# Experts of a mixture layer: a second feature block straight to PE in fp32, and GpSimd's share of the low parts cut to the first five

## The chip, the cores and the metric

The kernel runs on one core of a Trainium2 chip. The metric is the device time of one execution in microseconds. Before the change the median of three runs is 3178.11 us (3177.04 to 3182.73).

The engines are named as in the profile: PE is TensorE (matmuls; PEld is its loading of weights), DVE is VectorE, ACT is ScalarE, POOL is GpSimd, and SP issues nearly all DMAs from one queue in order.

## The reference

The model is a first block (a state-space mixer and a mixture of experts) followed by a second block of two layers, on 512 tokens of 1024 features, all in fp32. The change touches the experts of the first block alone:

```python
def expert_choice_ffn(xn, router_w, w_gate, w_up, w_down):
    ...
    gate, idx = lax.top_k(aff, cap)
    xg = jax.vmap(lambda xs, ix: xs[ix])(xn, idx)
    hid = jax.nn.silu(jnp.einsum('becd,edf->becf', xg, w_gate)) * jnp.einsum('becd,edf->becf', xg, w_up)
    y = jnp.einsum('becf,efd->becd', hid, w_down) * gate[..., None].astype(xn.dtype)
    ...
```

There are 16 experts; each picks 64 tokens. Each has three weight matrices of 1024 x 1024 in fp32, w_gate, w_up and w_down. All 48 matrices are read once: 48 x 4 MB.

## The kernel before

**Precision.** Most matmuls are made of fp32r operands, a shorter form of fp32. So that nothing is lost, an fp32 operand is split into two parts: high = the operand cast to fp32r (by ACT), low = operand minus high (by DVE or GpSimd). Products of the parts are added up in PSUM.

**Stages.** A mixer, its output projection with the router (`w_o`, `route`), then the experts (`experts`, line 1086), then the second block (`b2_entry`, `layer`). The order of the instructions on each engine is made by a planner that simulates the program when the kernel is built (`schedule_with_timeline_sim`); in the experts no order is written out by hand, apart from a dependency that holds a few early loads behind the gather of the first tokens.

**The experts.** The loop in `experts` takes expert after expert. For expert e it calls `hidden(e)` (gate and up matrices, silu, product), then `finish(e - 1)`, which calls `down` for the expert before. After every odd expert `pair_rows` and, after experts 1, 5, 9 and 13, `combine` add the results of the pairs to the residual rows `h`. For every even expert `xs_pair` transposes the gathered tokens of the next pair and `gather` fetches those of the one after it.

**One matrix, eight feature blocks.** A matrix is taken in eight blocks k = 0 to 7 of 128 input features x 1024 output features, 512 KB each (`moe_mm`, line 1007). All 384 blocks of the stage come in one fixed order. `moe_load` (line 929) issues the load of the next block into one of 19 raw buffers in rotation: seven `mraw`, three `raw`, four `PT`, four in `rawx`, one in `moewk`. A load waits on SP's queue until the last reader of its buffer is done.

`moe_w` (line 943) prepares a block. A block whose k is in `DIRECT` (line 26: k = 2) is handed to PE as it is. Any other is split: ACT casts the high part (L955) and an engine subtracts for the low part (L957). That engine is GpSimd for the first five split blocks and for every ninth after them (`MPOOL`, line 27), else DVE. High and low parts have four buffers each, three `whi`/`wlo` and one `mwhi`/`mwlo`. Then the next load is issued.

`moe_mm` has the matmuls. The stationary operand of a split block holds 64 columns of high and 64 columns of low parts of the tokens (`XS` for gate and up, `HS` for down), so that two matmuls on each half of 512 output features give all four products: one with the block's high part (L1017), one with its low part (L1018). A direct block has one plain fp32 matmul on each half (L1015), whose stationary operand is the 64 tokens in fp32 (`XD` for gate and up, the tile `hs` for down), and it issues its next load after them. In the trace each plain fp32 matmul has two records. Both kinds add into the same PSUM rows:

```python
                if wl is None:
                    nc.tensor.matmul(pp[q][0:64], X32[k], wh[:, c], start=False, stop=False)
                    continue
                nc.tensor.matmul(pp[q], X[:, k], wh[:, c], start=k == 0, stop=False)
                nc.tensor.matmul(pp[q], X[:, k], wl[:, c], start=False, stop=k == 7)
            if wl is None:
                self.moe_load()
```

At the end of a gate or up matrix ACT copies PSUM out (L1031, L1032) and PE multiplies by a constant matrix J (L1035), which adds the high and low rows and transposes. At the end of a down matrix ACT copies the low rows (L1055) and DVE adds them (L1056). `xs_pair` transposes (L996) and splits the tokens (ACT L1003, DVE L1004), and ACT copies block 2 of them to `XD` (L1001).

Of the kernel before, what the change touches and what calls it, by code (L numbers as in the profile page):

```python
# [22 lines left out]
MRAW = 7  # L23
AFTER = (0, 1, 2, 3)
RAWS = MRAW + 12
DIRECT = (2,)
MPOOL = 9
GROUPS = (1, 5, 9, 13)
CAP = 64
EPS = 1e-6  # L30
# [7 lines left out]
class Net:  # L38
# [904 lines left out]
    def moe_w(self, *key):  # L943

        nc = self.nc
        got, raw = self.raws.pop(0)
        assert got == key
        if key[2] in DIRECT:
            return raw, None
        n = self.cw  # L950
        self.cw += 1
        P, tag, bufs = (self.wp, "w", 3) if n % 4 < 3 else (self.mw, "mw", 1)
        hi = P.tile([128, 1024], F32R, name=tag + "hi", tag=tag + "hi", bufs=bufs)
        lo = P.tile([128, 1024], F32R, name=tag + "lo", tag=tag + "lo", bufs=bufs)
        nc.scalar.copy(hi, raw)  # L955
        eng = nc.gpsimd if n < 5 or n % MPOOL == MPOOL - 1 else nc.vector
        eng.tensor_tensor(lo, raw, hi.bitcast(F32), OP.subtract)  # L957
        self.moe_load()
        return hi, lo
# [27 lines left out]
    def xs_pair(self):  # L987

        nc, mo = self.nc, self.mo2
        XS = [mo.tile([128, 8, 128], F32R, name="XS%d" % i, tag="XS", bufs=3) for i in range(2)]  # L990
        XD = mo.tile([128, max(1, len(DIRECT)), 2, 64], F32, name="XD", tag="XD", bufs=2)
        for q in range(2):
# [5 lines left out]
            ks = slice(4 * q, 4 * q + 4)  # L998
            for j, k in enumerate(DIRECT):
                if k // 4 == q:  # L1000
                    nc.scalar.copy(XD[:, j], p4[:, k % 4])  # L1001
            for i in range(2):
                nc.scalar.copy(XS[i][:, ks, 0:64], p4[:, :, i])  # L1003
                nc.vector.tensor_tensor(XS[i][:, ks, 64:128], p4[:, :, i], XS[i][:, ks, 0:64].bitcast(F32), OP.subtract)  # L1004
        return [(XS[i], {k: XD[:, j, i] for j, k in enumerate(DIRECT)}) for i in range(2)]

# [16 lines left out]
    def hidden(self, e, X):  # L1023
# [19 lines left out]
        V.tensor_tensor(HS[:, :, 64:128], s3, HS[:, :, 0:64].bitcast(F32), OP.subtract)  # L1043
        return HS, {k: s3[:, k] for k in DIRECT}

# [1030 lines left out]
```

## Time and profile before

| | before |
|---|---|
| median of three runs | 3178.11 us (3177.04 to 3182.73) |
| the profiled execution | 3183.61 us, of which the span from the first to the last instruction 3181.8 us |
| mean granted TensorE clock over the span | 0.981 of full speed |
| PE, DVE, ACT, POOL busy | 96%, 71%, 50%, 12% of the span |
| split blocks in the experts | 336, of which 294 low parts by DVE and 42 by POOL |
| direct blocks in the experts | 48 |

The profile shows one execution. An engine's busy time is the union of its records; matmuls are pipelined, so the records of neighbours overlap and a matmul's duration is longer than what it adds to the time. An arrow `<-` behind an idle time names the instruction whose end released the one that waited. A tile's name stands without its buffer's number; `mm<-wlo,XS` is a matmul into the tile `mm` that reads `wlo` and `XS`.

### The profile page before, as it was taken

How to read it: one execution, taken by the hardware profiler on the slowest of the kernel's cores; microseconds unless marked ns; L12 is line 12 of the kernel's file. 1: busy time of each engine (PE TensorE's matmuls, PEld its weight loads, DVE VectorE, ACT ScalarE, POOL GpSimd, SP SyncE). 2: the span in 40 equal slices, each digit the busy share in tenths (PEclk: the TensorE clock that was granted, in tenths of full speed). 3: DMA queues.
4: the chain of work that ended last, by engine and by line, in shares of the span. 5: the costliest groups of instructions: out<-in, count | busy, mean ns of one | idle time of the engine just before them, and what ended most of it. 6: DMA issues, size and time to landing. Idle time of an engine off the chain costs nothing. (4 is left out here: it accounts for less than half of the span.)

```text
span 3181.8 us, 43471 instructions
## 1 busy us (share of the span) xinstructions
PE 3039.0 (96%) x16242; PEld 2477.6 (78%) x16242; DVE 2247.8 (71%) x3782; ACT 1587.9 (50%) x2711; POOL 379.9 (12%) x295
## 2 busy tenths in 40 slices
PE   7999999969999999699999999999999999999998
PEld 4888777756655666678787789998878777789986
DVE  7778665468988888777565488873676655688854
ACT  6445432228766776365353435551465444445541
POOL 1454200032112121200011000000000011000000
PEclk9999999979999999899999999999999999999999
DMA  5112245549999997311215333332312224333332
GB/s 196 54 47 71 83 143 192 198 179 396 374 345 342 350 370 271 101 62 58 87 56 166 97 117 99 109 105 93 106 54 74 76 93 148 100 106 107 107 100 79
DMA packets 140781, 470.05 MB, mean 148 GB/s; under 512 B 16269, under 2 KB 20365, under 8 KB 140569
## 3 DMA queue, kind: packets, MB, share of 16 engines
q1 hardware_dynamic: 139416, 463.08, 41.7%
q0 software_dynamic: 1152, 4.19, 0.4%
q8 instruction: 127, 2.08, 0.3%
q14 instruction: 86, 0.70, 0.1%
HBM read 456.71 MB, written 10.50 MB: 147 GB/s over the span
## 5 line engine op out<-in xcount | busy, mean ns | idle before, releaser
L107 DVE TENSOR_TENSOR wlo<-raw,whi 128x1024 fp32r<-128x1024 f32 (+4 forms) x340 | 379.9, 1120 | 306.4 <-ACT whi L106 305.0
L106 ACT CAST whi<-raw 128x1024 fp32r<-128x1024 f32 (+4 forms) x340 | 317.6, 936 | 416.7 <-PE mm L116 165.0
L115 PE MATMUL mm<-xTh,whi 128*128 128x512 f32 (+2 forms) x880 | 344.7, 392 | 5.6 <-ACT P L1245 2.6
L116 PE MATMUL mm<-xTh,wlo 128*128 128x512 f32 (+3 forms) x880 | 341.3, 388 | 0.0
L117 PE MATMUL mm<-xTl,whi 128*128 128x512 f32 (+2 forms) x880 | 339.1, 386 | 0.4 <-DVE xTl L267 0.2
L115 PE MATMUL mm<-whi,xTh 128*128 128x512 f32 (+1 forms) x536 | 208.1, 390 | 2.5 <-DVE zt L562 2.1
L116 PE MATMUL mm<-whi,xTl 128*128 128x512 f32 (+1 forms) x536 | 208.2, 389 | 0.5 <-DVE xTl L1150 0.5
L117 PE MATMUL mm<-wlo,xTh 128*128 128x512 f32 (+1 forms) x536 | 204.7, 387 | 0.0
L115 PEld LDWEIGHTS mm<-xTh,whi 128*128 128x128 f32 (+1 forms) x880 | 165.8, 188 | 46.5 <-ACT P L1245 4.2
L117 PEld LDWEIGHTS mm<-xTl,whi 128*128 128x128 f32 (+1 forms) x880 | 165.4, 188 | 36.9 <-DVE xTl L267 1.5
L116 PEld LDWEIGHTS mm<-xTh,wlo 128*128 128x128 f32 (+1 forms) x880 | 165.9, 189 | 34.3 <-issue 1.4
L1018 PE MATMUL mm<-wlo,XS 128*128 128x512 f32 x336 | 114.3, 413 | 18.0 <-DVE wlo L957 11.7
L1409 POOL TENSOR_TENSOR ql<-q,qh 128x512 fp32r<-128x512 f32 x16 | 20.7, 1291 | 853.0 <-ACT qh L1408 853.0
L115 PEld LDWEIGHTS mm<-whi,xTh 128*128 128x128 f32 x536 | 102.1, 191 | 23.4 <-DVE zt L562 2.5
L116 PEld LDWEIGHTS mm<-whi,xTl 128*128 128x128 f32 x536 | 102.1, 191 | 20.3 <-DVE xTl L1150 1.0
L117 PEld LDWEIGHTS mm<-wlo,xTh 128*128 128x128 f32 x536 | 102.0, 190 | 19.7
L957 DVE TENSOR_TENSOR wlo<-mraw,whi 128x1024 fp32r<-128x1024 f32 x82 | 108.6, 1341 | 8.9 <-ACT whi L955 7.7
L1017 PE MATMUL mm<-whi,XS 128*128 128x512 f32 x336 | 111.2, 406 | 0.9 <-ACT whi L955 0.9
L955 ACT CAST whi<-mraw 128x1024 fp32r<-128x1024 f32 x96 | 97.7, 1049 | 15.2 <-PE mm L1017 12.5
L1245 ACT ACTIVATE P<-mm,smv 128x512 f32<-128x512 f32 x128 | 88.1, 690 | 31.2 <-DVE P L1533 16.1
L107 DVE TENSOR_TENSOR flo<-fs,fhi 128x1024 fp32r<-128x1024 f32 x80 | 97.6, 1220 | 5.7 <-ACT fhi L106 4.6
L116 PE MATMUL mm<-whi,hl 128*128 128x512 f32 x248 | 96.6, 390 | 0.0
(827 smaller groups left out, 8620.3 us busy)
## 6 DMA issues: line engine op xcount, KB each, us to landing
raw<-w_f SPq DMA_DIRECT2D x92, 512.0 KB
raw<-w_gate SPq DMA_DIRECT2D x68, 512.0 KB
mraw<-w_gate SPq DMA_DIRECT2D x52, 512.0 KB
mraw<-w_down SPq DMA_DIRECT2D x49, 512.0 KB
araw<-ada SPq DMA_DIRECT2D x48, 512.0 KB
mraw<-w_up SPq DMA_DIRECT2D x43, 512.0 KB
rawu<-w_f SPq DMA_DIRECT2D x40, 512.0 KB
PT<-w_up SPq DMA_DIRECT2D x30, 512.0 KB
```

The lines of the kernel that those rows point to most:

```text
L106: nc.scalar.copy(hi[:, :n], raw[:, :n])
L107: nc.vector.tensor_tensor(lo[:, :n], raw[:, :n], hi[:, :n].bitcast(F32), OP.subtract)
L115: mm(out, ah, bh, start=first, stop=False)
L116: mm(out, al, bh, start=False, stop=False)
L117: mm(out, ah, bl, start=False, stop=last)
L955: nc.scalar.copy(hi, raw)
L957: eng.tensor_tensor(lo, raw, hi.bitcast(F32), OP.subtract)
L1017: nc.tensor.matmul(pp[q], X[:, k], wh[:, c], start=k == 0, stop=False)
L1018: nc.tensor.matmul(pp[q], X[:, k], wl[:, c], start=False, stop=k == 7)
L1245: nc.scalar.activation(P, s, AF.Exp, bias=v[:, 8 + i:9 + i], accum_out=v[:, 16 + i:17 + i])
L1409: nc.gpsimd.tensor_tensor(ql, q, qh.bitcast(F32), OP.subtract)
```

## The change

`DIRECT` names a second block, k = 6, so that two of the eight blocks of each matrix go to PE unsplit. `xs_pair` and `hidden` take the list as it is, so `XD` grows to two blocks for each expert of a pair, and ACT makes one more copy for each pair. The constant `MPOOL` goes, and with it GpSimd's every ninth low part: GpSimd keeps the first five, and all others are DVE's.

```diff
-DIRECT = (2,)
-MPOOL = 9
+DIRECT = (2, 6)
...
         nc.scalar.copy(hi, raw)
-        eng = nc.gpsimd if n < 5 or n % MPOOL == MPOOL - 1 else nc.vector
+        eng = nc.gpsimd if n < 5 else nc.vector
         eng.tensor_tensor(lo, raw, hi.bitcast(F32), OP.subtract)
         self.moe_load()
         return hi, lo
```

## Rows read from the trace of the kernel before

**Rows 1.** The page, busy time of each engine over the span.

```profile
PE 3039.0 (96%) x16242; PEld 2477.6 (78%) x16242; DVE 2247.8 (71%) x3782; ACT 1587.9 (50%) x2711; POOL 379.9 (12%) x295
```

**Rows 2.** Busy time by stretches: us, busy (instructions) per engine, PEclk, DMA share, GB/s.

```profile
core 0: us, PE busy (x) PEld busy (x) DVE busy (x) ACT busy (x) POOL busy (x), PEclk, DMA share, GB/s
720.00:760.00 40.00, 39.51 (x190) 28.01 (x189) 35.07 (x37) 33.23 (x44) 9.06 (x4) 1.00 1.01 394
705.00:1275.00 570.00, 534.88 (x2284) 357.03 (x2284) 486.04 (x490) 412.21 (x510) 114.62 (x45) 0.99 0.92 347
```

**Rows 3.** Timeline, PE, 899 to 917 us: start, us, what.

```profile
899.78 0.63 PE L1017 MATMUL mm<-whi,HS 128*128 128x512 f32 x2
...
903.05 0.63 PE L1018 MATMUL mm<-wlo,XS 128*128 128x512 f32 x2
903.62 1.93 PE L1015 MATMUL mm<-mraw,XD 128*64 128x512 f32 x4
905.48 0.72 PE L1017 MATMUL mm<-whi,XS 128*128 128x512 f32 x2
...
906.51 0.63 PE L1017 MATMUL mm<-whi,XS 128*128 128x512 f32 x2
...
909.32 1.10 PE L1017 MATMUL mm<-whi,XS 128*128 128x512 f32 x4
911.89 0.73 PE L1018 MATMUL mm<-wlo,XS 128*128 128x512 f32 x2 [1.48 <-DVE wlo L957]
...
915.81 1.10 PE L1035 MATMUL aux<-J,moewk 128*128 128x64 f32 x8
916.73 0.71 PE L1017 MATMUL mm<-whi,XS 128*128 128x512 f32 x2
```

**Rows 4.** Groups of PE, 705 to 1275 us: busy, mean ns, idle before and its releasers.

```profile
L1018 PE MATMUL mm<-wlo,XS 128*128 128x512 f32 x336 | 114.3, 413 | 18.0 <-DVE wlo L957 11.7 <-POOL wlo L957 5.8
...
L1035 PE MATMUL aux<-J,moewk 128*128 128x64 f32 x512 | 64.0, 272 | 1.3 <-ACT moewk L1031 1.3
L1018 PE MATMUL mm<-wlo,HS 128*128 128x512 f32 x168 | 56.6, 408 | 2.8 <-DVE wlo L957 2.1 <-POOL wlo L957 0.7
...
L1018 PE MATMUL mm<-mwlo,XS 128*128 128x512 f32 x112 | 38.5, 415 | 3.1 <-DVE mwlo L957 1.6 <-POOL mwlo L957 1.3
...
L1015 PE MATMUL mm<-mraw,XD 128*64 128x512 f32 x48 | 23.2, 605 | 0.0
L1082 PE MATMUL aux<-yh,oht 128*128 128x512 f32 x56 | 20.8, 406 | 2.2 <-DVE h L1115 1.2 <-ACT yh L1066 1.1
...
L1018 PE MATMUL mm<-mwlo,HS 128*128 128x512 f32 x56 | 18.9, 414 | 1.5 <-DVE mwlo L957 1.4
...
L996 PE MATMUL aux<-ident,moewk 128*128 128x128 f32 x64 | 10.2, 295 | 4.9 <-DMA moewk<-xf_scratch,idx 4.9
...
L1071 PE MATMUL aux<-posT,s 16*64 16x512 f32 x32 | 8.6, 612 | 0.0
...
L976 PE MATMUL aux<-vals,OH 128*128 128x6 f32 x28 | 4.4, 261 | 0.0
```

**Rows 5.** Timeline of POOL, DVE and PE at two GpSimd subtracts.

```profile
907.95 2.80 POOL L957 TENSOR_TENSOR wlo<-PT,whi 128x1024 fp32r<-128x1024 f32 x1 [10.82 <-ACT whi L955]
...
908.80 3.04 DVE L957 TENSOR_TENSOR wlo<-PT,whi 128x1024 fp32r<-128x1024 f32 x1 [0.30 <-ACT whi L955]
...
1020.93 5.71 POOL L957 TENSOR_TENSOR wlo<-mraw,whi 128x1024 fp32r<-128x1024 f32 x1 [11.42 <-ACT whi L955]
...
1026.69 2.07 PE L1018 MATMUL mm<-wlo,XS 128*128 128x512 f32 x4 [3.95 <-POOL wlo L957]
```

**Rows 6.** DVE's subtracts in the experts: two groups, and one with min/median/max ns.

```profile
L957 DVE TENSOR_TENSOR wlo<-mraw,whi 128x1024 fp32r<-128x1024 f32 x82 | 108.6, 1341 | 8.9 <-ACT whi L955 7.7 <-ACT hs L1038 1.0
...
L957 DVE TENSOR_TENSOR mwlo<-moewk,mwhi 128x1024 fp32r<-128x1024 f32 x4 | 8.9, 2228 | 1.1 <-ACT mwhi L955 1.1
...
L957 DVE TENSOR_TENSOR wlo<-mraw,whi x82: 1203/1216/3427, 714.4 to 1270.6; 128x1024 fp32r<-128x1024 f32 x82
```

**Rows 7.** What SP's queue waited for, 705 to 1275 us: total us, times, longest.

```profile
SPq L941 <- PE mm L1015: 57.3, 37, 5.3
```

## The prediction, made before the changed kernel had run

> **What bounds the kernel now.** I read the page's busy shares first. PE is busy for 96% of the span, DVE for 71%, GpSimd for 12% [rows 1]. But a share over the whole span says little here: the change touches the experts alone, so I went on to the stretch of 705 to 1275 us, in which all 384 blocks of the experts' weights are used [rows 2]. There PE is busy for 534.9 of 570 us, DVE for 486.0, ACT for 412.2, GpSimd for 114.6. The reader is to see two things in that row: PE is the bound, with little room, and DVE comes close behind, close enough to make PE wait.
>
> Next, what one block costs PE. Matmuls overlap in the records, so I count from start to start, not by durations. Seven pairs of ordinary matmuls lie between 899.78 and 903.05 us [rows 3]: 3.27 / 7 = 0.467 us a pair, 0.2335 us each. A **split block** has four of them (high and low part, two halves): 0.934 us. A **direct block** stands between a pair that starts at 903.05 and two pairs that end at 906.51: 3.46 us, less three pairs of 0.467, leaves 2.06 us. Its own four records take 1.86 us (903.62 to 905.48); the other 0.2 us are at its two edges, where weights aren't loaded ahead. So a direct block costs PE more than two split ones.
>
> The Trainium skill, "FP8 and Floating Point Precision", section "TensorE Precision Notes", says that true fp32 takes four passes through the array. That speaks against the change, which spends PE time where PE is the bound; four passes for two fp32 matmuls against one pass for each of four fp32r ones would be a factor of two, and by that alone a block would add 0.934 us. The trace agrees and shows 0.2 us on top [rows 3].
>
> Then PE's account of the stretch [rows 4]. The matmuls on the low parts stand in four groups, 336 + 168 + 112 + 56 = 672, and there are as many on the high parts: 1344 x 0.2335 = 313.8 us. Forty-eight direct blocks (k = 2 of 16 experts and three matrices): 98.9. The 512 matmuls with J, eight of which take 0.92 us (915.81 to 916.73) [rows 3]: 58.9. The combine has 56 with yh and as many with yl: 26.2. Three small groups are busy for 8.6 + 10.2 + 4.4 us with overlap; I take 18. Sum 516. **So PE waits for about 54 of the 570 us.** The idle time recorded ahead of the matmuls on the low parts adds up to 16.8 us released by DVE and 7.8 by GpSimd [rows 4], 24.6 of the 35.1 us (570 - 534.9) of recorded idle, or 70%. I spread the 54 alike: 38 us are waits for a low part (26 by DVE, 12 by GpSimd), 16 are others.
>
> Why DVE is late: its subtract takes 1216 ns in the median but up to 3427 [rows 6]. The long ones lie beside GpSimd's: one of 3.04 us starts inside a GpSimd subtract of 2.80 us, and PE then stands for 1.48 us; elsewhere GpSimd needs 5.71 us for one block and PE stands for 3.95 us [rows 3, 5]. The ten groups of DVE's low parts (294 of them; the first and the last are shown) are busy for 390.0 us in sum [rows 6]; at 1216 ns they would take 357.5. So 32.5 us of DVE's time is lost beside GpSimd.
>
> **The change, part by part.** *Block 6 direct.* Forty-eight more direct blocks in place of split ones: 48 x (2.06 - 0.934) = **+54 us** of PE work, all of it on the path that sets the end. ACT loses 48 casts and gains eight small copies (XD for block 6), DVE loses subtracts; none of this ends last by itself, it counts only through PE's waits.
>
> *GpSimd.* It now makes the low parts of blocks n < 5 and of every ninth; 37 of the latter go. Of the 336 - 48 = 288 split blocks left, DVE makes 283, before 294. DVE's busy time: 486.0 - 32.5 - 11 x 1.216 = 440 us. Over a stretch of some 590 us its free time grows from 84 to 150 us. Also, between two direct blocks there are now three split ones at most, not seven. DVE falls behind by 1.216 - 0.934 = 0.28 us a split block: 0.85 us over three, 2.0 over seven, and catches up in the direct block.
>
> *What of the waits goes.* Those on GpSimd, 12 us, go whole. Of the 26 us on DVE I take three quarters, 20; what stays is where DVE has bursts of other work (the pair's rows, the combine's sums). Of the other 16 us I take 2. **Gain 34, cost 54: +20 us.** The bounds: nothing of the waits goes, +54; all 54 go, 0.
>
> *The loads.* A direct block's raw buffer comes free only when PE has read it, and its next load is issued there, in order, with all later loads behind it on SP's queue. SP already waits 57.3 us in all for such matmuls in 37 places [rows 7], twice that after. I cost it at nothing: with 19 raw buffers the loads run about 19 x 1.48 us ahead (570 us / 384 blocks), and a block held some 3 us longer uses little of it. If that cover were gone, PE would wait for bytes; the third rival prices it.
>
> *The order of work* is set by the planner, which sees other costs now; elsewhere some microseconds either way, in the range.
>
> The sum is made against the profiled execution, 3183.6 us (span 3181.8 and 1.8 around it), which lies 5.5 us over the median of the three runs, 3178.1. I add the 20 us to the median: **3198 us**.
>
> **The rivals.** *One: all waits for low parts go.* With 38 us and some 10 of the others gone, the cost is 54 - 48 = +6 us or less: 3178 to 3184, no change. For it: DVE's free time nearly doubles. Against it: three blocks in a row still outrun DVE.
>
> *Two, faster: the edges of the direct blocks cost nothing new,* because they fall where PE stood anyway. Then a block adds 1.86 - 0.934 = 0.93 us, 44.5 in all, and with all 54 us of waits gone the time is 10 us lower: 3168. It decides from the point at which the waits that go exceed the work added. Against it: the edges show at a direct block without any wait beside it [rows 3].
>
> *Three, much slower: the waits stay.* The direct blocks hold raw buffers, SP's queue stops twice as often, and of the extra 57 us [rows 7] a part reaches PE while the waits on DVE shrink little: +40 to +60, 3218 to 3238.
>
> *Four: the stretch is bound by transfers.* Then PE's waits are for bytes in disguise, the added PE work fills them, and the time stays at 3178. Against it: in 720 to 760 us the queues moved 394 GB/s, and at that rate the 384 blocks (201.3 MB) need 511 us, not 570 [rows 2]. The Trainium skill, "SBUF — State Buffer", section "A bandwidth-pool intuition that's wrong", names about 358 GB/s as the way from HBM to a core and calls HBM almost always the bottleneck; by that the blocks would take 562 us, nearly the whole stretch. The row shows more than this figure, so the row decides.
>
> **How the numbers follow.** A run of this kernel can tell about 0.2%, 6.4 us, from no change. Forecast (+8 to +34): 0.62. Rival three: 0.12. Rival one: 0.16. Rival four: 0.03. Rival two: 0.07. Slower is the first two, 0.74; same rivals one and four, 0.19; faster 0.07. The range leaves out rival two, the half of rival three that is above 3218 and the planner's odd microseconds: 3178 to 3218.
>
> **What would show it.** Right: 96 direct blocks at about 2.06 us each from start to start; DVE's subtracts all near 1216 ns after the first few; GpSimd nearly idle in the stretch; the idle time ahead of the matmuls on low parts down to a third or less; the stretch some 20 us longer, all else alike. Wrong: a stretch not longer, or one that grew by 50 with the waits on DVE as before, or waits for loads ahead of casts.

## The result, and the profile after

The changed kernel takes 3212.61 us (median of four runs, 3212.37 to 3212.96), the kernel before 3180.42 us beside it. The ratio is 1.0101, with a 95% interval of 1.0088 to 1.0112: **slower by 32 us**. The forecast was 20 us slower, with a range that reached to 3218.

First, where the time went. From the first matmul on a split block to the start of the last one, the experts took 562.9 us before (710.7 to 1273.6 us of the span) and take 595.2 us now (708.6 to 1303.9). That is +32.3 us. What comes after that point took 1908.2 us before and takes 1906.6 now. The two profiled executions lie only 29.0 us apart (3183.6 and 3212.6), as the one of the kernel before is 3.2 us over its median; ahead of the experts the changed kernel is 2.1 us shorter. So all of the loss is in the experts, and the rest of this text stays there.

The busy shares of the page of the changed kernel, against [rows 1]:

```profile
PE 3084.7 (96%) x16242; PEld 2462.1 (77%) x16242; DVE 2196.3 (68%) x3771; ACT 1545.8 (48%) x2671; POOL 274.2 (9%) x258
```

PE gained 46 us of busy time, DVE lost 51, GpSimd 106. The work moved as planned. Next the stretches, with the columns of [rows 2]:

```profile
core 0: us, PE busy (x) PEld busy (x) DVE busy (x) ACT busy (x) POOL busy (x), PEclk, DMA share, GB/s
720.00:760.00 40.00, 40.00 (x173) 24.66 (x172) 29.25 (x34) 28.63 (x39) 0.96 (x1) 1.00 1.00 390
840.00:880.00 40.00, 40.00 (x172) 24.19 (x171) 30.15 (x37) 26.43 (x37) 0.94 (x1) 1.00 0.93 338
1160.00:1200.00 40.00, 38.55 (x143) 21.87 (x143) 25.93 (x27) 21.91 (x31) 0.00 (x0) 0.91 0.92 324
1200.00:1240.00 40.00, 36.63 (x128) 19.59 (x127) 25.72 (x24) 23.68 (x28) 0.00 (x0) 0.91 0.87 322
705.00:1305.00 600.00, 585.19 (x2284) 345.91 (x2284) 437.70 (x480) 370.20 (x471) 9.45 (x9) 0.98 0.89 329
```

The last two stretches of 40 us in the kernel before:

```profile
1160.00:1200.00 40.00, 36.90 (x151) 23.73 (x150) 34.65 (x31) 29.59 (x35) 8.29 (x3) 1.00 0.96 362
1200.00:1240.00 40.00, 37.13 (x157) 24.43 (x155) 33.79 (x28) 28.59 (x35) 9.12 (x3) 1.00 0.97 367
```

The reader is to see three things. In 720 to 760 and 840 to 880 us PE is busy for 40.00 of 40 us: no recorded wait is left there. In 1160 to 1200 and 1200 to 1240 us that is no longer so, and there the granted clock is 0.91 of full speed, where the kernel before had 1.00 in both. And over the stretch DVE is busy for 437.7 us, near the 440 of the forecast.

The new block, on PE's timeline (start, us, what):

```profile
903.89 0.63 PE L1017 MATMUL mm<-wlo,HS 128*128 128x512 f32 x2
904.45 1.93 PE L1014 MATMUL mm<-mraw,hs 128*64 128x512 f32 x4
906.31 0.72 PE L1016 MATMUL mm<-whi,HS 128*128 128x512 f32 x2
...
907.34 0.63 PE L1016 MATMUL mm<-whi,XS 128*128 128x512 f32 x2
```

From 903.89 to 907.34 us are 3.45 us; less three pairs of 0.467 they leave 2.05 us, which matches [rows 3]. DVE's subtract, with its shortest, median and longest time in ns, against [rows 6]:

```profile
L956 DVE TENSOR_TENSOR wlo<-mraw,whi x76: 1206/1220/1227, 729.4 to 1296.8; 128x1024 fp32r<-128x1024 f32 x76
```

No subtract of this group takes over 1227 ns now that GpSimd is out of the way (the longest was 3427). The Trainium skill, "SBUF — State Buffer", section "SBUF: two separate sides", says that a DVE instruction with two inputs in SBUF and a GpSimd instruction that reads SBUF exclude each other, the later one standing until the other is done; the traces agree, in this kernel by the absence of long subtracts, and in the first experiment by their return.

The groups of PE in the experts, against [rows 4] (L1016 has the high parts, L1017 the low ones, L1014 the direct blocks):

```profile
L1016 PE MATMUL mm<-whi,XS 128*128 128x512 f32 x288 | 101.5, 416 | 3.2 <-ACT whi L954 3.2
L1017 PE MATMUL mm<-wlo,XS 128*128 128x512 f32 x288 | 97.7, 403 | 1.4 <-DVE wlo L956 1.4
...
L1016 PE MATMUL mm<-whi,HS 128*128 128x512 f32 x144 | 52.8, 416 | 1.8 <-ACT whi L954 1.8
L1017 PE MATMUL mm<-wlo,HS 128*128 128x512 f32 x144 | 51.2, 405 | 2.9 <-DVE wlo L956 2.9
L1014 PE MATMUL mm<-mraw,XD 128*64 128x512 f32 x96 | 47.9, 622 | 0.0
L1016 PE MATMUL mm<-mwhi,XS 128*128 128x512 f32 x96 | 33.9, 418 | 1.2 <-ACT mwhi L954 1.2
L1017 PE MATMUL mm<-mwlo,XS 128*128 128x512 f32 x96 | 33.0, 408 | 1.1 <-DVE mwlo L956 1.1
```

The idle time ahead of the matmuls on low parts fell from 25.4 us in all [rows 4] to 5.4. But ahead of those on high parts it rose: 3.2 + 1.8 + 1.2 = 6.2 us, all released by a cast on ACT, where the kernel before had 1.9 us in two groups:

```profile
L1017 PE MATMUL mm<-whi,XS 128*128 128x512 f32 x336 | 111.2, 406 | 0.9 <-ACT whi L955 0.9
L1017 PE MATMUL mm<-mwhi,HS 128*128 128x512 f32 x56 | 18.6, 407 | 1.0 <-ACT mwhi L955 1.0
```

This is the new wait, and the forecast didn't have it. One case of it on the timeline of ACT and PE (other engines left out):

```profile
1230.81 0.60 ACT L1037 ACTIVATE hs<-aux 128x512 f32<-128x512 f32 x1 [4.33 <-PE aux L1034]
...
1231.14 0.63 PE L1016 MATMUL mm<-mwhi,XS 128*128 128x512 f32 x2
1231.61 0.63 PE L1017 MATMUL mm<-mwlo,XS 128*128 128x512 f32 x2
1231.81 1.05 ACT L954 CAST mwhi<-mraw 128x1024 fp32r<-128x1024 f32 x1 [0.39 <-PE mm L1016]
1232.76 1.04 ACT L954 CAST whi<-moewk 128x1024 fp32r<-128x1024 f32 x1
...
1233.85 0.73 PE L1016 MATMUL mm<-whi,XS 128*128 128x512 f32 x2 [1.62 <-ACT whi L954]
1235.30 0.81 PE L1017 MATMUL mm<-wlo,XS 128*128 128x512 f32 x2 [0.72 <-DVE wlo L956]
1236.05 3.49 PE L1014 MATMUL mm<-mraw,XD 128*64 128x512 f32 x4
...
1241.43 0.39 PE L1016 MATMUL mm<-mwhi,HS 128*128 128x512 f32 x1
```

ACT starts the casts of `mwhi` and `moewk` only at 1231.81 and 1232.76. The first waited for PE to free its buffer, which PE reads from 1231.14 on (0.39 us recorded), and before that ACT had stood for 4.33 us in front of an activation whose input PE hadn't made yet. And the order is turned round: the block in `moewk` is the one that PE needs next, at 1232.2, while it reads the new `mwhi` only at 1241.43. In ACT's queue the cast of the later block stands in front of the cast that PE waits for. PE ends its pair at about 1232.2, waits 1.62 us for the high part and 0.72 us for the low part. **Then the direct block that follows takes 3.49 us instead of 1.93**: PE runs at the lower of its two clock levels, 1.2 instead of 2.4 GHz. By the records of the granted clock, PE spent 17.1 us of the experts at half clock, against 3.4 us before; half of the difference, 6.8 us, is lost time by estimate.

SP's queue, against [rows 7]:

```profile
SPq L940 <- PE mm L1014: 122.5, 84, 5.3
```

The waits for direct blocks doubled, as said, but no cast and no split block's matmul waited for a load of the experts' weights: the cover held.

### The profile page after: what moved, and what is told of

It is laid out like the page before. It is cut to its first block, busy times and chain, and to the rows that moved or that the text cites. A ratio compares the mean times of both kernels' runs of the same rounds, so it can differ in the third digit from the quotient of the medians.

```text
span 3210.5 us, 43285 instructions
## 1 busy us (share of the span) xinstructions
PE 3084.7 (96%) x16242; PEld 2462.1 (77%) x16242; DVE 2196.3 (68%) x3771; ACT 1545.8 (48%) x2671; POOL 274.2 (9%) x258
## 5 line engine op out<-in xcount | busy, mean ns | idle before, releaser
L956 DVE TENSOR_TENSOR wlo<-mraw,whi 128x1024 fp32r<-128x1024 f32 x76 | 91.5, 1221 | 26.6 <-ACT whi L954 25.8
L1016 PE MATMUL mm<-whi,XS 128*128 128x512 f32 x288 | 101.5, 416 | 3.2 <-ACT whi L954 3.2
L1017 PE MATMUL mm<-wlo,XS 128*128 128x512 f32 x288 | 97.7, 403 | 1.4 <-DVE wlo L956 1.4
L954 ACT CAST whi<-mraw 128x1024 fp32r<-128x1024 f32 x80 | 82.2, 1048 | 34.2 <-PE mm L1016 32.1
L116 PE MATMUL mm<-wlo,hh 128*128 128x512 f32 x248 | 95.8, 389 | 0.0
```

The source lines that it names most:

```text
L116: mm(out, ah, bl, start=False, stop=last)
```

## The experiments

All kernels below change only the experts. The table has for each its median, the ratio to the kernel before with its 95% interval, and from its profiled execution the length of the experts' stretch (from the first to the last start of a matmul on a split block), the idle time ahead of matmuls on low and on high parts, and the time at half clock (spells that begin in the stretch). These four columns are of one execution; in two kernels it lies well off the median, with five pairs 3.5 us above it (3208.4), with the copies two behind 5.5 us below (3155.3). The first two cuts below are against the kernel before, the others against the changed kernel.

```
kernel                         us      ratio (95%)              stretch   low   high  half clock
before                         3180.4                            562.9   25.4   1.9    3.4
the change                     3212.6  1.0101 (1.0088..1.0112)   595.2    5.4   6.2   17.1
block 6 direct alone           3200.3  1.0065 (1.0051..1.0079)   584.3    6.0   0.9    6.8
GpSimd's share alone           3163.4  0.9949 (0.9935..0.9962)   547.1   11.8   3.4    3.4
blocks 1 and 5                 3208.6  1.0091 (1.0077..1.0105)   587.3    5.2   2.9    3.4
change, five pairs             3204.9  1.0072 (1.0059..1.0086)   587.9    3.0   0.5   13.7
change, copies behind casts    3204.4  1.0074 (1.0060..1.0088)   588.4    3.7   5.5   10.2
GpSimd's alone, five pairs     3170.3  0.9967 (0.9955..0.9979)   554.0   12.6   1.9    0.0
GpSimd's alone, two behind     3160.9  0.9936 (0.9922..0.9951)   541.1    9.4   6.3    0.0
half of block 6                3166.4  0.9954 (0.9939..0.9969)   547.3    5.5   1.3    0.0
change, every twelfth          3210.7  1.0089 (1.0075..1.0102)   589.6    8.5   0.7    3.4
change, every eighteenth       3212.8  1.0105 (1.0090..1.0121)   595.4    5.1   5.8   17.1
no direct block, GpSimd out    3162.6  0.9945 (0.9931..0.9958)   546.8   31.3   2.1    0.0
GpSimd's alone, one behind     3159.9  0.9935 (0.9921..0.9948)   541.9    7.8   5.7    3.4
```

### The two halves of the change, each alone

Block 6 direct, GpSimd as before:

```diff
-DIRECT = (2,)
+DIRECT = (2, 6)
```

> Block 6 direct, GpSimd keeps every ninth low part (32 of the 37 that the change took from it). Theory (PE's added work of some 51 us is paid in full, and what the change won back are waits for low parts, most of them made by GpSimd): PE pays the 51 us, and the waits beside GpSimd stay in good part, so 10 to 15 us slower than the changed kernel, some 3222 to 3227 us, and DVE subtracts of 2 to 3 us are seen again. Rival (the direct blocks alone remove the waits, GpSimd doesn't matter): as the changed kernel, 3209 to 3215 us.

Block 2 alone, GpSimd out:

```diff
-        eng = nc.gpsimd if n < 5 or n % MPOOL == MPOOL - 1 else nc.vector
+        eng = nc.gpsimd if n < 5 else nc.vector
```

> Only block 2 direct as before, GpSimd takes no low parts beyond the first five. Theory (GpSimd's subtracts cost PE waits, of its own 12 us and of DVE's beside it): no added work for PE, DVE's busy time about as before (37 subtracts of 1.22 us more, 36 us less of delay), waits down by 5 to 15 us: 3165 to 3175 us. Rival (DVE becomes the bound once it takes all low parts): 3180 us or more, and the waits for low parts stay above 35 us.

Block 6 alone costs 20 us and GpSimd's share alone wins 16: the first theory fell, for the direct block without GpSimd's part is *faster* than the whole change, by 12 us. Together the two halves should have cost 4 us if they had nothing to do with each other; they cost 32. In the kernel with block 6 alone, DVE's subtracts are long again beside GpSimd's (one group, shortest, median, longest in ns), yet PE hardly waits for low parts (groups of PE: L1017 high, L1018 low):

```profile
L957 DVE TENSOR_TENSOR wlo<-rawx,whi x37: 1211/1220/3431, 723.6 to 1274.2; 128x1024 fp32r<-128x1024 f32 x37
```

```profile
L1017 PE MATMUL mm<-whi,XS 128*128 128x512 f32 x288 | 98.5, 415 | 0.2 <-ACT whi L955 0.2
L1018 PE MATMUL mm<-wlo,XS 128*128 128x512 f32 x288 | 94.3, 402 | 2.6 <-DVE wlo L957 2.6
...
L1018 PE MATMUL mm<-wlo,HS 128*128 128x512 f32 x144 | 50.6, 408 | 3.1 <-DVE wlo L957 3.1
```

So two direct blocks give DVE enough room that even subtracts of 3.4 us come in time. With GpSimd's share alone, the same waits fall too, to less than half (groups of PE: L1016 high, L1017 low; three of the eight groups):

```profile
L1017 PE MATMUL mm<-wlo,XS 128*128 128x512 f32 x336 | 110.6, 406 | 5.9 <-DVE wlo L956 5.9
L1016 PE MATMUL mm<-whi,XS 128*128 128x512 f32 x336 | 110.3, 406 | 2.7 <-ACT whi L954 2.7
...
L1017 PE MATMUL mm<-mwlo,XS 128*128 128x512 f32 x112 | 37.4, 408 | 3.9 <-DVE mwlo L956 3.7
```

**Both halves buy the same waits.** Idle time ahead of low parts is 25.4 us before, 6.0 with the one, 11.8 with the other and 5.4 with both. Once block 6 is direct, taking GpSimd out has nothing left to buy.

### What a direct block costs

```diff
                 if wl is None:
+                    if k == 6 and q == 1:
+                        continue
                     nc.tensor.matmul(pp[q][0:64], X32[k], wh[:, c], start=False, stop=False)
```

> As the changed kernel, but block 6 is multiplied for the first half of the output features alone: the second plain fp32 matmul of block 6 is left out in all 48 matrices, every other instruction stays. Theory (PE is the bound and a plain fp32 matmul costs it 0.86 us on the path): 48 x 0.86 = 41 us faster at most, 30 to 43 us with waits coming back, 3170 to 3183 us. Rival (part of the direct blocks' time is covered by waits that stand there anyway): less than 20 us faster, 3193 us or more.

The 48 matmuls that are left out were worth 3212.6 - 3166.4 = 46 us, 0.96 us each: more than the 41 us "at most", since the time at half clock went as well (17.1 to 0.0 us, half of it 8.6 us). Without that some 38 us are left, nine tenths of the 41. Hardly anything covers a direct block; PE pays nearly all of it. The rival is out.

From the other side, no block direct at all, and GpSimd out:

```diff
-DIRECT = (2, 6)
+DIRECT = ()
```

> No block direct, GpSimd takes the first five low parts: PE has 48 direct blocks less than with block 2 alone (48 x 1.06 = 51 us less work), DVE 48 subtracts of 1.22 us more, some 555 us of work. Theory (a direct block pays as long as DVE is the later engine, and costs its full price once PE is): DVE becomes the bound, its 555 us and some gaps make a stretch of 565 to 590 us, 3180 to 3205 us, slower than block 2 alone (3163.4). Rival (PE's work alone counts): 30 to 50 us faster than 3163.4, 3113 to 3133 us.

Neither came: 3162.6 us, the same as with block 2 direct (3163.4). The stretch in the columns of [rows 2], and PE's largest group on low parts:

```profile
705.00:1255.00 550.00, 507.08 (x2284) 363.49 (x2282) 534.87 (x575) 457.65 (x550) 9.00 (x8) 1.00 0.95 360
```

```profile
L1017 PE MATMUL mm<-wlo,XS 128*128 128x512 f32 x384 | 133.1, 424 | 21.6 <-DVE wlo L956 21.1
```

DVE is busy for 534.9 of 550 us, so it is the bound, as the theory had it; but its work was put 20 us too high. PE's 507.1 us of busy time are 26 us less than the 532.8 with block 2 direct, and the idle time ahead of low parts is 31.3 us instead of 11.8. **With GpSimd out, already the first direct block costs PE just what it saves in waits**; the second only costs.

### Where the last 12 us come from

The change lies 12 us above block 6 alone, though GpSimd's subtracts delay nobody there. In the table high parts and half clock differ: 6.2 against 0.9 us, and 17.1 against 6.8 us (half of it lost). That is 5.3 + 5.2 us, less 0.6 us on low parts, about 10 of the 10.9 us by which the stretches differ. What I tried to tell apart is whether these are due to GpSimd's share itself or to the order in which the planner puts ACT's work. First the same work with other direct blocks:

```diff
-DIRECT = (2, 6)
+DIRECT = (1, 5)
```

> As the changed kernel, but blocks 1 and 5 are the direct ones instead of 2 and 6. Same work on every engine, another order by the planner. Theory (the 12 us above the forecast come from casts that stand behind waiting copies in ACT's queue, which is a matter of the planner's order): the time moves by more than 6 us, either way. Rival (the whole cost is PE's work): within 3 us of the changed kernel, 3210 to 3216 us.

3208.6 us, 4 us below the change, with intervals that overlap: neither outcome clearly, though the stretch of its profiled execution is 8 us shorter with the same work on each engine. Then more room between ACT and PE:

```diff
-MRAW = 7
+MRAW = 5
...
-        P, tag, bufs = (self.wp, "w", 3) if n % 4 < 3 else (self.mw, "mw", 1)
+        P, tag, bufs = (self.wp, "w", 3) if n % 5 < 3 else (self.mw, "mw", 2)
```

> As the changed kernel, with five pairs of buffers for high and low parts instead of four, and 17 raw buffers instead of 19. Theory (what is left of PE's waits are high parts cast late): casts run one block further ahead, PE's waits for high and low parts fall by half, 10 to 15 us faster than the changed kernel, 3198 to 3203 us. Rival (the waits left stand outside this rotation, or the time is PE's work alone): 3210 to 3216 us. If the loads were near their limit, fewer raw buffers would show as waits for DMAs.

The idle time ahead of high parts goes to 0.5 us and that ahead of low parts to 3.0, and the time falls by 8 us, a little short of the theory. It was at half clock for 13.7 us all the same. Then ACT's copies out of PSUM, held behind the casts of the next two blocks; `moe_w` takes its blocks from a list that is prepared two ahead. The edit also holds back loads that fall due while a direct block stands in that list, until that block's matmuls (not shown in the cut):

```diff
...
+        while len(self.prep) < 1 + LOOK and self.raws:
+            self.prep.append(self.prepare())
+        got, hi, lo = self.prep.pop(0)
...
-            nc.scalar.copy(g[:, 0:512], pp[0])
+            c0 = nc.scalar.copy(g[:, 0:512], pp[0])
             nc.scalar.copy(g[:, 512:1024], pp[1])
+            self.behind(c0, self.cast)
```

> As the changed kernel, but blocks are prepared two ahead in the program, and the copy of a gate or up matrix out of PSUM on ACT is made to depend on the latest of those casts, so that it can't stand in front of them in ACT's queue. Theory (in the changed kernel some 11 us are waits for high parts whose casts stood behind such a copy, and the lower clock after them): the stretch loses them, 8 to 14 us faster than the changed kernel, 3199 to 3205 us, and the direct blocks run at full clock throughout. Rival (the wait only moves, PE then stands before the products with J): 3210 us or more.

The time came into the expected range, 3204.4, but not for the expected reason. The group with most idle time ahead of high parts (L1027), and two stretches with a lower clock:

```profile
L1027 PE MATMUL mm<-whi,HS 128*128 128x512 f32 x144 | 54.0, 425 | 3.9 <-ACT whi L962 3.9
```

```profile
1040.00:1080.00 40.00, 37.64 (x139) 21.67 (x138) 27.04 (x26) 25.87 (x31) 0.00 (x0) 0.96 0.94 342
1080.00:1120.00 40.00, 40.00 (x138) 23.31 (x137) 28.92 (x31) 20.70 (x25) 0.00 (x0) 0.91 0.85 311
```

High parts still cost 5.5 us of idle time, and the clock still falls, to 0.91 in one stretch. So the copies were not the whole of it, and this run doesn't show that they were the cause. Last, GpSimd's share in steps:

```diff
+MPOOL = 12
...
-        eng = nc.gpsimd if n < 5 else nc.vector
+        eng = nc.gpsimd if n < 5 or n % MPOOL == MPOOL - 1 else nc.vector
```

> As the changed kernel, but GpSimd takes every twelfth low part besides the first five, 24 in all (none in the changed kernel, 32 when block 6 alone was changed). PE's work is the same. Rival (with two direct blocks GpSimd's share itself is worth the 12 us between those two): a line between them, 3203 to 3204 us. Theory (low parts aren't late in either; the 12 us are where the planner's order lets ACT hold casts back, and the clock after such stops): no line, the time anywhere from 3198 to 3213 us, and in step with the time at half clock in the experts, 7 us in the kernel with 32 and 17 us in the changed one.

The same with `MPOOL = 18`:

> As the changed kernel, but GpSimd takes every eighteenth low part besides the first five, 16 in all. Rival (GpSimd's share itself is worth the 12 us): on the line between 3212.6 (none) and 3200.3 (32), so 3206 to 3207 us. Theory (the planner's order and the clock): off the line by 3 us or more in this run or in the one with 24, and in step with the time at half clock.

Every eighteenth gives 3212.8 us, 6 us off the line and just the changed kernel's time, with its waits for high parts (L1017 high, L1018 low here; three of eight groups) and its 17.1 us at half clock:

```profile
L1017 PE MATMUL mm<-whi,XS 128*128 128x512 f32 x288 | 100.7, 415 | 3.2 <-ACT whi L955 3.2
L1018 PE MATMUL mm<-wlo,XS 128*128 128x512 f32 x288 | 96.9, 404 | 1.4 <-DVE wlo L957 1.4
...
L1017 PE MATMUL mm<-whi,HS 128*128 128x512 f32 x144 | 52.7, 420 | 1.8 <-ACT whi L955 1.8
```

So with 16 more subtracts on GpSimd the 12 us are still lost: they aren't in proportion to GpSimd's share. Every twelfth is off the line too, by 7 us, but doesn't bear the theory out whole: it is at half clock for 3.4 us and its stretch is 5.6 us shorter than the changed kernel's, 2.6 us off the line, yet its time is only 2 us lower. In its profiled execution 1911.8 us come after the stretch, where the changed kernel has 1906.6. The granted clock tells why: from 1340 to 3190 us it was at half for 27.3 us there, in the changed kernel for 13.7, and half of the difference is 6.8 us. So this run's time says little about the experts, and the case against the line rests on every eighteenth.

What follows: in the stretch, some 10 of the 10.9 us are waits for high parts and time at half clock, as the traces show. They also show what ACT does there. The raw buffers and those of the high parts rotate in a fixed order, so each cast can be matched to its block. In the changed kernel 5.8 of the 6.2 us ahead of high parts stand in front of five blocks whose cast was queued behind that of a later block, as at 1232.76 above, and all four spells at half clock begin within 3 us of such a wait. With every eighteenth they are the same five blocks (5.4 of 5.8 us), with block 6 alone it is one (0.7 of 0.9 us), with every twelfth none. The planner's order of the casts is thus where the two kernels part. No edit that only puts them back into block order was run, so its price isn't shown by itself, and why the planner chose this order stays open. With the copies behind the casts, 1.6 of the 5.5 us are of this kind; the others have another cause.

### A version that beats both

GpSimd's share alone (3163.4 us) beats both kernels. Two variants of it, with five pairs of buffers, and with the copies behind the casts of two blocks ahead:

> Block 2 alone direct, GpSimd takes the first five low parts, and five pairs of buffers for high and low parts with 17 raw buffers. Theory (PE's waits left there come from bursts of other work on DVE and ACT, which one more pair covers): 5 to 12 us faster than the same with four pairs (3163.4), 3151 to 3158 us. Rival (DVE's work of some 500 us in a stretch of 547 is what is left, depth doesn't help): 3160 to 3166 us.

> Block 2 alone direct, GpSimd takes the first five low parts, and the copies out of PSUM made to follow the casts of two blocks ahead. Theory (copies ahead of casts in ACT's queue cost PE here too, though less, since ACT waits 30 us for PE there and 55 in the changed kernel): 2 to 8 us faster than 3163.4. Rival (with DVE as the next bound the casts are not what is late): within 3 us of 3163.4, or slower by what PE then waits before the products with J.

Five pairs lose 7 us there by the medians (3170.3), against theory and rival. With the copies behind the casts the median is 2.5 us lower (3160.9), which the intervals don't tell apart from none; its runs scatter from 3155.3 to 3164.8. With one block ahead:

> Block 2 alone direct, GpSimd the first five, copies out of PSUM made to follow the cast of one block ahead instead of two. Theory (the casts behind the copies matter little there): within 4 us of the kernel with two ahead (3160.9) and of that without (3163.4). Rival (one block ahead is the better balance, the products with J wait less): 3 us or more faster than 3160.9.

3159.9 us, the same within the scatter: **21 us below the kernel before, beside which it ran, and 53 below the change**, ratio 0.9935. In this kernel and the one with two ahead the experts' stretch is 541 to 542 us.

## Why the prediction held, and what it missed

The direction and the largest term were right. The loss is 32 us where 20 were forecast, and the time lies 5 us inside the far end of the range.

**The price of block 6** was right: 54 us by a direct block of 2.06 us; the trace after has 2.05, and half of the block, left out, took 46 us away, of them 8.6 by the clock.

**The waits for low parts** were right in size: 32 of 38 us were to go (84%), and the recorded idle time fell from 25.4 to 5.4 us (79%). What was wrong is whom the forecast credited. It gave 12 us to GpSimd's leaving and the rest to DVE's room; the experiments show that either edit alone removes most of them. The step should have asked what each edit buys once the other is made. That would have priced the part on GpSimd at nothing beside the direct block, and shown it as a gain of 16 us without it.

**"Of the other 16 us I take 2"** is the term that failed. With 54 us of cost and about 30 us won on low parts (79% of 38) the stretch would have grown by 24 us; it grew by 32.3. So the other waits, put at 2 us less, came out some 8 us more. The runs show what it was: 4.3 us more idle time ahead of high parts, and 6.8 us lost at half clock, less some 2 us of idle time elsewhere. ACT stood longer for PE (ahead of the copies out of PSUM 55.3 us instead of 39.1), and at five blocks the cast that PE needed was queued behind one of a later block. I had costed ACT's edits at nothing, "only through PE's waits", and named no wait of that kind.

**The loads** stayed covered, as predicted.

**The rivals.** One (all waits go) was nearly right on low parts and fell on the others. Two (the edges cost nothing) fell with the 2.05 us. Three (+40 to +60) had the wrong mechanism: no load was late. Four (bound by transfers) is out. The kernel with copies held two behind, in the columns of [rows 2]:

```profile
1040.00:1080.00 40.00, 40.00 (x169) 26.96 (x168) 36.55 (x37) 31.07 (x37) 0.00 (x0) 1.00 1.01 400
705.00:1250.00 545.00, 526.71 (x2283) 358.45 (x2281) 486.00 (x528) 413.45 (x510) 9.75 (x8) 1.00 0.95 363
```

It moves 400 GB/s for 40 us, and its 541 us for 201.3 MB are fewer than the 562 us that the forecast worked out from the Trainium skill's figure ("SBUF — State Buffer", "A bandwidth-pool intuition that's wrong"). The measurement decides: the transfers don't bind.

## What to carry to other kernels

When two edits of one change relieve the same wait, price each with the other made: their gains don't add, but their costs do. Work moved onto the engine that is the bound is paid in full, and its relief elsewhere is worth at most the waits that the bound engine still has, counted from start to start. And an engine that is relieved may stand longer at the head of its queue for the bound engine, so look at what is queued behind such waits, and in which order, before calling the relief free.

## What the runs showed of the hardware that was not expected

A stop of PE can cost more than itself, but a stop alone doesn't decide it. In the changed kernel, after 1.62 and 0.72 us of waiting within four microseconds, the next direct block ran in 3.49 instead of 1.93 us at 1.2 GHz. In the same kernel PE stood for 2.17 us up to 1018.6 us, and the granted clock stayed at full speed, 2.4 GHz:

```profile
1016.00:1022.00 6.00, 3.83 (x12) 1.51 (x11) 5.95 (x7) 1.93 (x3) 0.28 (x1) 1.00 0.99 374
```

With the copies behind the casts, on the other hand, PE is busy for 40.00 of 40 us from 1080 to 1120 us, and the clock is 0.91 there. In the experts of kernels with the same work on PE the time at half clock was between 3.4 and 17.1 us. It went to zero in four kernels, one of them with 31.3 us of idle time ahead of low parts, in many short waits. What brings the clock down in one place and not in another is open.
